# Values of two attentions projected 512 columns at a time, with the work around them re-ordered

## The chip, the cores and the metric

The kernel runs on one core of one Trainium2 chip. The metric is device time in microseconds (us) from launch to end, the median of the runs of one launch each; lower is better. Five engines work beside each other and wait for one another by semaphores: TensorE (PE in the profile; PEld its weight loads), VectorE (DVE), ScalarE (ACT), GpSimd (POOL) and SyncE (SP), which here issues all DMAs.

## What is computed

Two layers over 512 tokens of width 1024, in float32. Layer A is differential attention (8 heads, each the difference of two softmaxes, with rotary positions and a block-causal mask), layer B is chunked band attention (16 heads, with a learned bias by distance). Each is followed by a SwiGLU FFN of hidden width 2816, and every sub-layer ends in a LayerNorm of alpha * x + sublayer(x).

```python
def diff_attention(x, w_qkv, ...):
    q, k, v = split(x @ w_qkv)                 # each 512 x 1024
    a = softmax(q1 k1) - lam * softmax(q2 k2)  # per head and 128-query block
    o = rms_norm(a @ v, subln_g) * (1 - lambda_init)
    return o @ w_o
def chunk_attention(x, k_band, v_band, ...):
    q = x @ w_q
    p = softmax(q k_band + bias[h])            # own chunk and 8 before
    return (p @ v_band) @ w_o
def reference(x, ...):
    for l in range(2):
        x = layer_norm(alpha * x + attention_l(x))
        x = layer_norm(alpha * x + (silu(x @ w_gate) * (x @ w_up)) @ w_out)
```

k and v of layer B come from one projection of x by `kv_w`.

## The kernel before, in words

**Precision.** Every product of a projection is made of three matmuls: each operand is split into a high part (rounded to fp32r by ScalarE, or a cast while a bank is read out) and a low part (the rest, by VectorE's or POOL's subtraction), and high x high, high x low and low x high are summed in one PSUM bank. `token_major` (L407) has activations stationary and weights moving, `feature_major` (L397, for q, k, gate and up) the other way round.

**Weights.** All weight chunks stand in one list (`order`, L290 to 342), each 512 KB, 1024 values in each of 128 partitions. Five raw buffers are loaded ahead by `fetch` (L350) in that order, on SP's queue. `take` (L385) hands out a chunk and lets the split run up to two chunks ahead (`AHEAD`, L41), with at most four split chunks alive (`NSPL`, L40); `free` (L391) releases one. A chunk's low part is made by VectorE, or by POOL where the plan says so (the later values of both attentions, the later k of B).

**PSUM.** Eight banks of 512 float32 columns, in four pairs by tag: `sc0`, `sc1`, `sm`, `pj`. A new tile of a tag takes the bank used longest ago and waits until its readers are done.

**Order on the engines.** Nothing is scheduled by the program: a model of times (`Model`, L98; `passed`, L184) keeps an estimate of when each tile is ready, and work of VectorE, ScalarE and POOL that hangs on TensorE is written into the program when the model's clock gets there (`later`, `chain`, `tick`). Each engine then runs its instructions in the order written.

**The attention loops.** `attention_a` (L1106) and `attention_b` (L1351) go through 32 units (8 heads or pairs of heads x 4 query blocks), each in steps by `STEPS` and `STEPS_B` (L50, L52): scores, then softmax on VectorE and ScalarE, then the transposes of the probabilities (`at`), then the product with the values (`o`, or `v` once per pair in B). Between steps `weave` (L247) puts in filler: `FA` and `FB` (L49, L53) say how many ns of filler at which step, and where a step's inputs are not ready by the model, filler is pulled forward. Filler is the list `FILL_A` or `FILL_B` (L327, L328): the projections of later q and k ("qk") and of the values ("v", `value_fill` L840), then the first half of the output projection (`project_out`, L456). Its first 36 matmuls (row tiles 0 and 1, k 0 to 5, in the `pj` banks) need no more than the heads that are done; those of row tiles 2 and 3 take the `sc0` banks of the scores and wait for `gate(-1)`, which is `done["s"]`, set at the last unit's scores (L1123, L1370). In A q and k of head h start no sooner than unit 4(h-2) is scored, and are turned by rotary tables, which sends them through a DMA within SBUF. In B, q and k of pair p are read out, and filler goes on, once unit 4(p-1) is scored (L1224).

**Values.** `value_quarter` (L819) projects 256 of the 1024 value columns: for each of four row tiles 8 k x 3 matmuls of 256 columns, two row tiles sharing one bank. Quarter 0 of A comes with the input's transposes (L993 to 1029), then q and k of head 0, then quarter 1 (L1031); quarters 2 and 3 are filler. In B quarter 0 comes between the first and second halves of q and k of pair 0 (L1232 to 1245), the other three are filler.

**Transposes.** `transpose_split` (L412) transposes one row tile of 128 tokens into two `sm` banks (8 transposes) and reads each out as high part (ScalarE), low part (VectorE) and, where an FFN follows, as a whole into `hb` (ScalarE). In `swiglu` (L529) those of row tiles 2 and 3 are put between the first matmuls of gate and up, as soon as their LayerNorm is done by the model; first halves (tokens 0 to 255) of hidden units 0 and 1 run in `sc0` and `sc1`, then their second halves, unit 0's in the two `pj` banks (L788).

Of the kernel before, what the change touches and what calls it, by code (L numbers as in the profile page):

```python
# [19 lines left out]
P = 128  # L20
# [32 lines left out]
FB = ((1780.0, 1360.0, 0.0), (630.0, 2250.0, 100.0), 12, (2600.0, 0.0, 5250.0))  # L53
# [80 lines left out]
def trunk(ctx, tc, x, a_w_qkv, a_lambda, a_subln_g, a_w_o, kv_w, b_w_q, b_rel_bias, b_w_o,  # L134
# [684 lines left out]
    def value_quarter(g, banks, name):  # L819

        ws = [take(f"{name}_{g}_{c}") for c in range(2)]

        def part(i):
            for t in (2 * i, 2 * i + 1):
                b = banks[i][:, (t % 2) * 256:(t % 2) * 256 + 256]
                for k in range(KT):
                    ts_ = slice(t * P, (t + 1) * P)
                    w_ = ws[k // 4]
                    token_major(b, xTh[:, k, ts_], xTl[:, k, ts_], w_[0][:, k % 4, :], w_[1][:, k % 4, :],
                                k == 0, k == KT - 1)  # L830
                    if t == NT - 1 and k % 4 == 3:
                        free(f"{name}_{g}_{k // 4}")
                    yield True
            for t in (2 * i, 2 * i + 1):
                act_e.copy(vt[t][:, g * 256:(g + 1) * 256], banks[i][:, (t % 2) * 256:(t % 2) * 256 + 256])
            if i:
                values_done[0] = g + 1
        return part(0), part(1)
# [61 lines left out]
    for t in range(NT):  # L900
# [5 lines left out]
        if t < 2:  # L906
            fetch()
# [85 lines left out]
    vbank = [b_[:, 0:256] for b_ in pair("va_ps0") + pair("va_ps1")]  # L993

    def first_values(t, c, w_):
        ts_ = slice(t * P, (t + 1) * P)
        for i, (x_, v_) in enumerate(((xTh, w_[0]), (xTl, w_[0]), (xTh, w_[1]))):
            for j in range(4):
                mm(vbank[t], x_[:, 4 * c + j, ts_], v_[:, j, :], start=(c == i == j == 0),
                   stop=(c == 1 and i == 2 and j == 3))  # L1000

    transpose_split(xin[0], 0)
    tick(True)
    w0 = take("va_0_0")
    tick(True)
    transpose_split(xin[1], 1)
    tick(True)
    w1 = take("va_0_1")
    tick(True)
    first_values(0, 0, w0)  # L1010
    first_values(1, 0, w0)
    transpose_split(xin[2], 2)
    tick(True)
    first_values(0, 1, w1)
    first_values(1, 1, w1)
    transpose_split(xin[3], 3)
    tick(True)
    state["ahead"] = AHEAD
    for t in (2, 3):
        for c, w_ in ((0, w0), (1, w1)):  # L1020
            first_values(t, c, w_)
    free("va_0_0")
    free("va_0_1")
# [3 lines left out]
    for t in range(NT):  # L1027
        act_e.copy(vt[t][:, 0:256], vbank[t])
    values_done[0] = 1
    now(qk_a(0))  # L1030
    now(value_fill(1, "va"))  # L1031
# [74 lines left out]
    def attention_a():  # L1106
# [3 lines left out]
        for i in range(nu + max(step[1] for step in STEPS if step[0] != "fill")):  # L1110
            rates = FA[0] if i < FA[2] else FA[1] if i < nu else FA[3]
            for kind, n in STEPS:
# [6 lines left out]
                if kind == "s":  # L1119
# [3 lines left out]
                    done["s"] = i == nu - 1  # L1123
# [114 lines left out]
    for i, _ in enumerate(v0[0]):  # L1238
        tick()
        if not vt and (there(xres[3], late=LATP) or i == 2 * KT - 1):  # L1240
            pre_b[1](None)
            for t in range(NT):
                vt.append(resid.tile([P, D], F32, tag="res", name=f"vb_{t}"))
# [195 lines left out]
```

## Time and profile before

| | us |
|---|---|
| median of 3 runs | 1223.04 (1220.2 to 1223.32) |
| the profiled execution | 1223.91 |
| its span, first to last instruction | 1222.1 |
| TensorE busy | 1188.6 (97%) |
| VectorE busy | 834.2 (68%) |
| ScalarE busy | 555.8 (45%) |
| POOL busy | 417.1 (34%) |

One execution was recorded. Its stages, by the timeline: input transposes, values, q and k of head 0 to 47.9 us; attention A to about 236; the rest of its output projection and LayerNorm to 259.7; FFN of A to 612.4; attention B's projections ahead of the loop to 651.3, its loop to 832.1, the rest of its output projection to 863.8; FFN of B to the end. Matmuls are pipelined, so the duration of one (some 0.28 us for 256 columns) is longer than the distance to the next; the distance is read from pieces of the chain or from starts.

### The profile page before, as it was taken

To read this page: it belongs to the slowest core of one execution; us is meant where nothing else is said; L and a number is where in the kernel's file an instruction comes from. 1 tells how busy PE (TensorE), PEld (TensorE's weight loads), DVE (VectorE), ACT (ScalarE), POOL (GpSimd) and SP (SyncE) were. 2 spreads that over 40 slices of the span, in tenths; PEclk is the share of its full clock that TensorE was granted. 3 is DMA by queue.
4 is the path that set the end of the run, shared out by engine and by line. 5 is a ranking of instruction groups with operands and counts; after the bars stand their busy time and mean duration, and the time that the engine had idled before them with its cause. 6 is when DMAs were issued, how large, how long until landed. Compare 5 with 4: busy or idle time off the path is not lost.

```text
span 1222.1 us, 20005 instructions
## 1 busy us (share of the span) xinstructions
PE 1188.6 (97%) x7640; PEld 1079.4 (88%) x7640; DVE 834.2 (68%) x1451; ACT 555.8 (45%) x1049; POOL 417.1 (34%) x410
## 2 busy tenths in 40 slices
PE   7999999999999999999999999999999999999997
PEld 7878897789999999888897988978899999998886
DVE  3588786587888887432655676775888888873327
ACT  3467666344544444322236576662444444433220
POOL 1126343513555663001213243113236665510022
PEclk9999999999999999999999999999999999999999
DMA  8444233543544443424254233225433333353321
GB/s 258 126 107 120 65 105 93 173 131 98 148 141 140 139 133 119 162 88 138 86 146 122 86 105 112 80 78 189 122 104 104 104 105 104 106 191 100 104 69 69
DMA packets 164193, 145.75 MB, mean 119 GB/s; under 512 B 6097, under 2 KB 137457, under 8 KB 164097
## 3 DMA queue, kind: packets, MB, share of 16 engines
q1 hardware_dynamic: 164096, 144.47, 39.2%
q8 instruction: 60, 0.98, 0.3%
q14 instruction: 37, 0.30, 0.1%
HBM read 127.63 MB, written 13.67 MB: 116 GB/s over the span
## 4 chain that ended last, share of the span: by engine, by line
PE 90%; DVE 5%; issue 1%; DMA 1%; ACT 1%; POOL 1%; SPq 0%; DVEq 0%; POOLq 0%; ACTq 0%
PE m L198 31%; PE c L198 5%; PE a L198 5%; PE b L198 5%; PE gu L198 5%; PE d L198 4%; PE va_ps L198 4%; PE vb_ps L198 4%; PE bq_ps L198 3%; PE bk_ps L198 3%; PE q_ps L198 3%; PE k_ps L198 3%; PE ob L198 2%; PE po L198 2%; PE sc_b L198 2%; PE pt_b L203 1%
## 5 line engine op out<-in xcount | busy, mean ns | idle before, releaser
L76 POOL TENSOR_TENSOR sums<-raw_u 128x512 f32<-128x512 f32 x38 | 49.0, 1290 | 184.0 <-DVE s3lo L76 166.6
L76 ACT ACTIVATE sg<-sg 128x512 f32<-128x512 f32 x38 | 24.0, 633 | 189.6 <-DVE sg L76 189.6
L76 POOL TENSOR_TENSOR lo_fo<-raw_fo,hi_fo 128x1024 fp32r<-128x1024 f32 x8 | 19.1, 2388 | 217.3 <-ACT hi_fo L76 217.3
L76 POOL TENSOR_TENSOR sums<-raw_g,sums 128x512 f32<-128x512 f32 x38 | 84.6, 2226 | 0.0
L76 DVE TENSOR_TENSOR m<-m,m 128x256 f32<-128x256 f32 x76 | 31.7, 417 | 57.9 <-PE m L198 57.9
L76 ACT CAST hi_fk<-raw_fk 128x1024 fp32r<-128x1024 f32 x28 | 29.4, 1052 | 76.1 <-PE d L198 71.1
L76 DVE TENSOR_TENSOR lo_fk<-raw_fk,hi_fk 128x1024 fp32r<-128x1024 f32 x28 | 33.9, 1221 | 26.9 <-ACT hi_fk L76 26.9
L76 POOL TENSOR_TENSOR sums<-sums,raw_g 128x512 f32<-128x512 f32 x38 | 49.7, 1308 | 4.0 <-DMA raw_g<-in_ffn_w_in_dram 1.2
L76 POOL TENSOR_TENSOR sums<-raw_g,raw_u 128x512 f32<-128x512 f32 x38 | 50.9, 1340 | 0.0
L76 DVE TENSOR_TENSOR s1lo<-sums,s1hi 128x1024 fp32r<-128x1024 f32 x38 | 47.6, 1252 | 0.0
L76 DVE TENSOR_TENSOR alo<-raw_g,ahi 128x1024 fp32r<-128x1024 f32 x38 | 47.0, 1236 | 0.0
L76 ACT CAST hi_fo<-raw_fo 128x1024 fp32r<-128x1024 f32 x16 | 16.9, 1054 | 64.5 <-PE d L198 64.5
L76 DVE TENSOR_TENSOR s3lo<-sums,s3hi 128x1024 fp32r<-128x1024 f32 x38 | 46.0, 1212 | 0.1
L76 ACT CAST s3hi<-sums 128x1024 fp32r<-128x1024 f32 x38 | 40.0, 1052 | 8.3 <-POOL sums L76 4.6
L198 PE MATMUL m<-T1h,s1hi 128*128 128x256 f32 x152 | 43.0, 283 | 0.0
L198 PE MATMUL m<-T1l,s1hi 128*128 128x256 f32 x152 | 43.0, 283 | 0.0
L198 PE MATMUL m<-T1h,s1lo 128*128 128x256 f32 x152 | 43.0, 283 | 0.0
L198 PE MATMUL m<-T2g,s1hi 128*128 128x256 f32 x152 | 43.0, 283 | 0.0
L198 PE MATMUL m<-T2b,s1hi 128*128 128x256 f32 x152 | 43.0, 283 | 0.0
L198 PE MATMUL m<-T2g,s1lo 128*128 128x256 f32 x152 | 43.0, 283 | 0.0
L198 PE MATMUL m<-T3h,s3hi 128*128 128x256 f32 x152 | 43.0, 283 | 0.0
L198 PE MATMUL m<-T3l,s3hi 128*128 128x256 f32 x152 | 43.0, 283 | 0.0
(612 smaller groups left out, 4772.4 us busy)
## 6 DMA issues: line engine op xcount, KB each, us to landing
raw_g<-in_ffn_w_in_dram SPq DMA_DIRECT2D x44, 512.0 KB, 4.0
raw_u<-in_ffn_w_in_dram SPq DMA_DIRECT2D x44, 512.0 KB, 5.2
raw_fk<-in_ffn_w_out_dram SPq DMA_DIRECT2D x28, 512.0 KB, 4.0
raw_fo<-in_ffn_w_out_dram SPq DMA_DIRECT2D x16, 512.0 KB, 3.7
skew<-extd SPq DMA_DIRECT2D x16, 320.0 KB, 5.9
raw_va<-in_a_w_qkv_dram SPq DMA_DIRECT2D x8, 512.0 KB, 4.8
raw_q<-in_a_w_qkv_dram SPq DMA_DIRECT2D x8, 512.0 KB, 5.1
raw_k<-in_a_w_qkv_dram SPq DMA_DIRECT2D x8, 512.0 KB, 4.7
```

The lines of the kernel that those rows point to most:

```text
L76: return issue(*args, **kwargs)
L198: nc.tensor.matmul(out_, lhsT, rhs, start=start, stop=stop)
L203: nc.tensor.transpose(out_, in_, ident)
```

## The change

Values are projected 512 columns at a time ("half") in both attentions: `values` takes the place of `value_quarter`, a half's weights come as four chunks of 2 k x 512 columns in place of two of 4 k x 256, and each row tile has a bank of its own. Half 0 of each attention is computed ahead of its loop, half 1 is filler after q and k of head or pair 4. Beside that:

- A's first values: the loads alternate x tile, value chunk four times, and the first values' matmuls (`value_piece`, chunk by chunk) are placed between the transposes of the four x tiles. No values lie between q and k of head 0 and the loop.
- B's first values are placed chunk by chunk too: chunks 0 and 1 for row tiles 0 to 2, with tile 3's transposes among them, then the second halves of q and k of pair 0, then the rest.
- `transpose_split` uses the `pj` banks, not `sm`, for row tile 3 where an FFN follows.
- `done["s"]` is set at the last unit's `at` step, not at its scores.
- `FILL_A` and `FILL_B` end with q and k of 5, 6 and 7; `FB` is lowered by some 10%.

```diff
-FB = ((1780.0, 1360.0, 0.0), (630.0, 2250.0, 100.0), 12, (2600.0, 0.0, 5250.0))
+FB = ((1600.0, 1250.0, 0.0), (550.0, 2050.0, 100.0), 12, (2600.0, 0.0, 5250.0))
...
-        for c in range(2):
-            chunk(f"{name}_{g}_{c}", w, 4 * c, 4, c0 + g * 256, 256, pool)
+        for c in range(4):
+            chunk(f"{name}_{g}_{c}", w, 2 * c, 2, c0 + g * HALF, HALF, pool)
...
-    FILL_A = [("qk", 1), ("qk", 2), ("qk", 3), ("qk", 4), ("v", 2), ("qk", 5), ("qk", 6), ("v", 3), ("qk", 7)]
-    FILL_B = [("qk", 2), ("v", 1), ("qk", 3), ("qk", 4), ("v", 2), ("qk", 5), ("qk", 6), ("v", 3), ("qk", 7)]
+    FILL_A = [("qk", 1), ("qk", 2), ("qk", 3), ("qk", 4), ("v", 1), ("qk", 5), ("qk", 6), ("qk", 7)]
+    FILL_B = FILL_A[1:]
     plan_values("va", w_qkv, 2 * D, 0)
     plan_qk_a(0)
-    plan_values("va", w_qkv, 2 * D, 1)
...
-            pt = bank("sm", f"xt_ps_{t}_{g}")
+            pt = bank("pj" if whole and t == NT - 1 else "sm", f"xt_ps_{t}_{g}")
...
+    def values(g, name, parts, bank_of):
+        ws = []
+        def part(ts):
+            banks = [bank_of(t) for t in ts]
+            for t, b in zip(ts, banks):
                 for k in range(KT):
+                    if k % 2 == t == 0:
+                        ws.append(take(f"{name}_{g}_{k // 2}"))
...
+            for t, b in zip(ts, banks):
+                act_e.copy(vt[t][:, g * HALF:(g + 1) * HALF], b)
...
+    def value_piece(b, t, c, w_):
+        ts_ = slice(t * P, (t + 1) * P)
+        for i, (x_, v_) in enumerate(((xTh, w_[0]), (xTl, w_[0]), (xTh, w_[1]))):
+            for j in range(2):
+                mm(b, x_[:, 2 * c + j, ts_], v_[:, j, :], start=(c == i == j == 0), stop=(c == 3 and i == 2 and j == 1))
     def value_fill(g, name):
-        banks = [bank("pj", f"{name}_ps{i}_{g}") for i in range(2)]
-        for p_ in value_quarter(g, banks, name):
+        for p_ in values(g, name, [[t] for t in range(NT)], lambda t: bank("pj", f"{name}_ps{t}_{g}")):
             yield from p_
...
-        if t < 2:
-            fetch()
+        fetch()
...
+    first_x(0)
+    first_w()
+    first_x(1)
+    first_values(0, 0)
+    first_w()
+    first_values(1, 0)
+    first_x(2)
+    first_values(0, 1)
+    first_values(1, 1)
+    first_w()
+    first_values(2, 0)
+    first_x(3)
+    first_values(2, 1)
+    for t in range(3):
+        first_values(t, 2)
+    first_w()
...
-    now(value_fill(1, "va"))
...
-                    done["s"] = i == nu - 1
...
+                if kind == "at":
+                    done["s"] = i - n == nu - 1
...
+    for c in range(2):
+        first_values_b(c, range(3))
+    if not vt:
+        last_tile()
     now(first)
+    for c in range(4):
+        first_values_b(c, range(3 if c < 2 else 0, NT))
+        free(f"vb_0_{c}")
...
-                    done["s"] = i == nu - 1
                     done["n"] = i + 1
                 elif kind == "at":
                     yield lambda: there(live[i - n][1])
+                    done["s"] = i - n == nu - 1
```

## Rows read from the trace of the kernel before

**Rows 1.** The page, part 1: busy us, share of the span, instructions.
```profile
PE 1188.6 (97%) x7640; PEld 1079.4 (88%) x7640; DVE 834.2 (68%) x1451; ACT 555.8 (45%) x1049; POOL 417.1 (34%) x410
```

**Rows 2.** Windows: stretch, length, busy us by engine, granted clock, DMA share, GB/s.
```profile
267.30:269.50 2.20, 0.25 (x2) 0.05 (x1) 2.14 (x3) 0.61 (x2) 0.00 (x0) 1.00 0.99 256
270.50:273.90 3.40, 3.40 (x18) 3.40 (x17) 2.06 (x4) 3.11 (x6) 0.92 (x1) 0.50 1.16 292
...
655.50:661.80 6.30, 4.95 (x25) 3.37 (x24) 4.03 (x15) 3.63 (x15) 1.79 (x4) 1.00 0.15 46
...
651.30:717.90 66.60, 65.25 (x383) 56.70 (x382) 45.67 (x127) 44.71 (x115) 23.04 (x36) 1.00 0.33 99
...
651.30:832.10 180.80, 176.47 (x1051) 155.65 (x1050) 128.16 (x345) 118.33 (x305) 52.69 (x90) 0.99 0.30 91
```

**Rows 3.** Waits of TensorE: us in total, times, longest.
```profile
PE xt_ps L203 <- DMA xin<-in_x_dram: 6.7, 2, 3.6
PE xt_ps L203 <- ACT hb L76: 3.9, 2, 2.0
PE ob L198 <- DVE klb_b L76: 2.6, 1, 2.6
...
PE sc L198 <- DMA ks<-ks: 1.7, 1, 1.7
```

**Rows 4.** The chain of waits in order of time: start, us, what.
```profile
25.53 5.58 PE q_ps L198 x24
...
36.69 11.39 PE va_ps L198 x96
...
236.36 10.88 PE oa_1a L198 x48
```

**Rows 5.** Timeline, both FFNs' beginnings: start, us, instruction, count [idle before <-releaser].
```profile
268.88 1.18 ACT L76 COPY hb<-xt_ps 128x512 f32<-128x512 f32 x2 [6.45 <-DVE xTl_a L76]
...
269.52 1.40 PE L203 MATMUL xt_ps<-ident,oa_x 128*128 128x128 f32 x8 [1.97 <-ACT hb L76]
...
271.65 1.07 ACT L76 CAST xTh_a<-xt_ps 128x512 fp32r<-128x512 f32 x2
...
272.99 1.18 ACT L76 COPY hb<-xt_ps 128x512 f32<-128x512 f32 x2 [0.27 <-DVE xTl_a L76]
...
277.48 0.28 PE L198 MATMUL gu<-xTh_a,hi_g 128*128 128x256 f32 x1
...
877.07 1.19 ACT L76 COPY hb<-xt_ps 128x512 f32<-128x512 f32 x2 [0.27 <-DVE xTl_b L76]
...
881.59 0.28 PE L198 MATMUL gu<-xTh_b,hi_g 128*128 128x256 f32 x1
```

**Rows 6.** Timeline of TensorE at the start; DMA traffic of the first 16 us.
```profile
12.11 1.05 PE L198 MATMUL va_ps<-lo_va,xTh_a 128*128 128x256 f32 x4
12.97 1.05 PE L198 MATMUL va_ps<-hi_va,xTh_a 128*128 128x256 f32 x4
...
DMA packets 4243, 4.46 MB, mean 279 GB/s; under 512 B 157, under 2 KB 3475, under 8 KB 4243
```

**Rows 7.** Timeline of TensorE where the second attention begins.
```profile
621.60 1.25 PE L203 MATMUL xt_ps<-ident,fx 128*128 128x128 f32 x8 [1.24 <-DVE xTl_b L76]
```

**Rows 8.** Instructions that split value weights: durations ns min/median/max, first and last start.
```profile
L76 POOL TENSOR_TENSOR lo_va<-raw_va,hi_va x4: 2374/2508/2840, 99.2 to 154.9; 128x1024 fp32r<-128x1024 f32 x4
...
L76 ACT CAST hi_vb<-raw_vb x8: 1033/1054/1063, 611.3 to 757.2; 128x1024 fp32r<-128x1024 f32 x8
```

**Rows 9.** Timeline after the last scores of the first attention, TensorE and VectorE.
```profile
218.71 0.50 PE L198 MATMUL oa<-hi_oa,oTh 128*128 128x512 f32 x1 [1.46 <-DVE nm L76]
...
220.69 0.75 DVE L76 SCALAR_TENSOR_TENSOR e<-e,c 128x512 f32<-128x512 f32 x1
```

**Rows 10.** Timeline of TensorE after the last scores of the second attention.
```profile
822.40 0.48 PE L198 MATMUL ob<-hi_ob,oTh 128*128 128x512 f32 x1
...
826.58 0.60 PE L203 MATMUL pt_b<-ident,e_b 128*128 128x128 f32 x4
```

More of the change, by code (lines that the diff above doesn't have):

```diff
@@ L817, in trunk @@
     values_done = [0]
[L819 to L825, printed above, removed]
+    def values(g, name, parts, bank_of):
[3 more added lines that the diff above has]
+            for t, b in zip(ts, banks):
                 for k in range(KT):
+                    if k % 2 == t == 0:
+                        ws.append(take(f"{name}_{g}_{k // 2}"))
                     ts_ = slice(t * P, (t + 1) * P)
-                    w_ = ws[k // 4]
-                    token_major(b, xTh[:, k, ts_], xTl[:, k, ts_], w_[0][:, k % 4, :], w_[1][:, k % 4, :],
+                    w_ = ws[k // 2]
+                    token_major(b, xTh[:, k, ts_], xTl[:, k, ts_], w_[0][:, k % 2, :], w_[1][:, k % 2, :],
                                 k == 0, k == KT - 1)
-                    if t == NT - 1 and k % 4 == 3:
-                        free(f"{name}_{g}_{k // 4}")
+                    if t == NT - 1 and k % 2:
+                        free(f"{name}_{g}_{k // 2}")
                     yield True
-            for t in (2 * i, 2 * i + 1):
-                act_e.copy(vt[t][:, g * 256:(g + 1) * 256], banks[i][:, (t % 2) * 256:(t % 2) * 256 + 256])
-            if i:
+            for t, b in zip(ts, banks):
+                act_e.copy(vt[t][:, g * HALF:(g + 1) * HALF], b)
+            if t == NT - 1:
                 values_done[0] = g + 1
-        return part(0), part(1)
+        return [part(ts) for ts in parts]
+    def value_piece(b, t, c, w_):
[3 more added lines that the diff above has]
+                mm(b, x_[:, 2 * c + j, ts_], v_[:, j, :], start=(c == i == j == 0), stop=(c == 3 and i == 2 and j == 1))
     def value_fill(g, name):
-        banks = [bank("pj", f"{name}_ps{i}_{g}") for i in range(2)]
-        for p_ in value_quarter(g, banks, name):
+        for p_ in values(g, name, [[t] for t in range(NT)], lambda t: bank("pj", f"{name}_ps{t}_{g}")):
             yield from p_
@@ L990, in trunk, with first_values, first_x, first_w @@
     lead = ap1.tile([HB, 255], F32, name="lead")
[L993 to L1017, printed above, removed]
-    state["ahead"] = AHEAD
[L1019 to L1023, printed above, removed]
+    vbank = pair("va_ps0") + pair("va_ps1")
+    wv = []
+    def first_values(t, c):
+        value_piece(vbank[t], t, c, wv[c])
+    def first_x(t):
+        transpose_split(xin[t], t)
+        tick(True)
+    def first_w():
+        wv.append(take(f"va_0_{len(wv)}"))
+        tick(True)
+    first_x(0)
[14 more added lines that the diff above has]
+    first_w()
+    state["ahead"] = AHEAD
+    for c in range(3):
+        first_values(3, c)
+        free(f"va_0_{c}")
+    for t in range(NT):
+        first_values(t, 3)
+    free("va_0_3")
     vt = []
@@ L1235, in trunk, with last_tile, first_values_b @@
     values_done[0] = 0
-    v0 = value_quarter(0, pair("vb_ps_0"), "vb")
-    vt = []
[L1238 to L1243, printed above, removed]
-    now(first)
-    now(v0[1])
+    vbank = pair("vb_ps_0") + pair("vb_ps_1")
+    wv, vt = [], []
+    def last_tile():
+        pre_b[1](None)
+        for t in range(NT):
+            vt.append(resid.tile([P, D], F32, tag="res", name=f"vb_{t}"))
+    def first_values_b(c, ts):
+        if len(wv) == c:
+            wv.append(take(f"vb_0_{c}"))
+        for t in ts:
+            value_piece(vbank[t], t, c, wv[c])
+            if not vt and there(xres[3], late=LATP):
+                last_tile()
+    for c in range(2):
+        first_values_b(c, range(3))
+    if not vt:
+        last_tile()
+    now(first)
+    for c in range(4):
+        first_values_b(c, range(3 if c < 2 else 0, NT))
+        free(f"vb_0_{c}")
+    for t in range(NT):
+        act_e.copy(vt[t][:, 0:HALF], vbank[t])
+    values_done[0] = 1
     now(qk_b(1))
@@ L1383, in attention_b @@
                     if qt == PREP_B:
-                        yield lambda: 2 * values_done[0] > p
+                        yield lambda: 4 * values_done[0] > p
                         split_values(p)
```

4 lines of the change are left out of this document (2 added, 2 removed).

## The prediction, made before the changed kernel was built or run

> **What bounds the kernel now.** The page first: TensorE is busy for 97% of a span of 1222.1 us [rows 1]. Matmuls overlap in those records, so what counts is where TensorE stands still and how far apart its matmuls start. The waits of TensorE give the first [rows 3]: 6.7 us on the first input tiles, 3.9 on ScalarE's copies out of the transposes' banks, 2.6 on `klb_b`, 1.7 on `ks`. The windows give what a wait costs afterwards [rows 2]: after 2.2 us of almost no TensorE work the clock granted from 270.5 to 273.9 is 0.50, the lower of its two levels (1.2 of 2.4 GHz). 3.4 us at half rate do 1.7 us less work. So a wait of about 2 us costs nearer 4. The chain of waits gives the second [rows 4]: 96 matmuls of 256 columns take 11.39 us, 118.6 ns each; 48 of 512 columns whose moving operand is a weight take 10.88 us, 226.7 ns each; 24 of a q or k projection take 5.58 us, 232.5 ns each.
>
> **Values in halves.** Per attention 4 quarters x 4 row tiles x 8 k x 3 = 384 matmuls of 256 columns become 192 of 512. 384 x 118.6 ns = 45.5 us; 192 x 226.7 ns = 43.5 us; 2.0 us less, as TensorE is the bound here. Both attentions: **-4.1 us**. I take 226.7, because the new matmul is built as that one is (activations stationary, weights moving). At 232.5 ns the gain would be 0.9 us each: bounds -4.1 and -1.8. The bytes stay the same; the 16 evacuations of 256 columns become 8 of 512 and lie on ScalarE, off the path.
>
> The Trainium skill (TensorE: Matmul & The Clock Gate, Back-to-back issue gap) puts isolated warm matmuls at N/2.4 + 2.5 ns apart, 109.2 and 215.8 ns. By that the gain would be an estimated 0.5 us per attention and the sum 3.1 us higher. The trace's spacing is wider by 9.4 ns at 256 columns and 10.9 at 512; no run here shows why, and I go by the rows.
>
> **The last transposes of each FFN's input.** Now both tiles' transposes (tiles 2 and 3) go to the two `sm` banks, so those of tile 3 wait until tile 2 has been read by ScalarE, VectorE and ScalarE again: `hb` copies from 268.88 for 1.18 us, transposes at 269.52 [rows 5]. With `pj` for tile 3 they start when TensorE gets there, at 267.3. Eight take 0.9 us (ending 268.2). Then the rest of unit 1's first half: 48 - 3 = 45 matmuls x 0.119 = 5.4 us, ending 273.6, with no wait ahead that brings the low clock. What is late next: the second halves write to those same `pj` banks, and start only when tile 3 has been read out. ScalarE's order is fixed (hb of tile 2, table load, silu, xTh at 271.65, hb at 272.99 for 1.18 in two copies), hangs on VectorE (the releaser in the row of 268.88) and not on the transposes, so the first bank is free at 273.6, the second at 274.2, and that one is needed 24 matmuls later. The second halves start at 277.48 now, at about 273.65 then: -3.8 us. The second FFN has the same: from 881.59 to about 877.75 (first of the `hb` copies done at 877.07 + 0.59): -3.8. Together **-7.7 us**. Bounds: none if the wait only moves to the `pj` bank with another fall of the clock (0); -7.9 if the copies come a little earlier.
>
> **First loads and first values.** TensorE runs without a break from the second input tile's transposes on; up to about 14.5 us at half rate (four matmuls in 12.97 - 12.11 = 0.86 us, 215 ns each, against 118.6 later [rows 6]). The new order keeps x0, a value chunk, x1, a value chunk, x2 at the head and slips one 512 KB load ahead of x3; at the mean 279 GB/s of the first 16 us [rows 6] this is 1.9 us, and x3 is wanted later too (more work lies ahead of it). I take 0; between -1 and +2 (x3 late). SP's queue has the same number of loads. Quarter 1 no longer lies between q0, k0 and the first scores, where its 11.4 us [rows 4] hid the rotary chain; the 48 matmuls of q1 and k1 (11.2 us) come there instead, being the first filler.
>
> **Start of the second attention.** The transposes of tile 3 wait 1.24 us on the `sm` banks after 3 matmuls [rows 7]; in the new order at least 6 of 512 columns (1.4 us, against 0.36) come between: **-0.9**. Bounds -1.2 and +1 (tile 2's low part is wanted by the third piece already).
>
> **The later half as filler: a new wait.** A half holds four weight chunks of which two are split ahead. The third and fourth are begun only when the first and second are taken; splitting one is 1.05 us on ScalarE and 2.5 us on POOL [rows 8]. From the start of the half the third is ready after some 4.5 us and wanted after 12 x 0.227 = 2.7 us of filler plus the attention matmuls woven in; the fourth after some 7 and wanted after 4.1. Behind the waiting matmul stands all of TensorE, since it works in order. Woven in it is 0.8 us per attention, in one piece 2.8; at best none. I take **+1.6** in all (0 to +5.6).
>
> **Filler in the second attention's loop.** Quarter 1 leaves the loop for the time ahead of it. Filler of pair p stops after its q until unit 4(p-1) is scored. Quarter 1 used to lie between k2 and q3 and carried the loop past the gates of p = 3 and 4. Without it units 6 and 10 run out of filler. Units without filler cost TensorE 6.30 - 4.95 = 1.35 us in 655.5 to 661.8 [rows 2]; and VectorE's 45.67 us in the first twelve units would stand in some 55 us in place of 66.6 once the quarter's 11.4 us go, 83% of the time, not 69, so that a late unit is made up more slowly. I take **+1.5** (0 to +5).
>
> **Score banks, last q and k.** In the first attention the output projection's second half of row tiles now waits for the last transposes, not the last scores. Now its first matmul stands 1.46 us on `nm` (218.71), after which 12 matmuls run before the last `e` is ready at 220.69 + 0.75 [rows 9]. Then nothing fills that gap: 12 x 0.227 = 2.7 us of work come later, 1.5 of waiting goes: +1.1. The last q and k come 1.3 us of filler earlier, which takes some 0.6 off the 1.7 us on `ks`: **+0.5** together (-3.4 if that wait falls short and the clock stays up; +3 with another fall). In the second attention the 2.6 us on `klb_b` is `ob`'s second bank waiting for the last k to be read out; k still comes straight ahead of it, so it stays. Of the 18 matmuls between 822.40 and 826.58 [rows 10] only what is left of the first row tiles can run: up to 15 x 0.227 = 3.4 us uncovered, some of it covered by filler left over from the gates. I take **+1.0** (-4.3 with the wait and its low clock gone, +5.1 with all uncovered and one more fall).
>
> **Sum.** -4.1 - 7.7 - 0.9 + 1.6 + 1.5 + 0.5 + 1.0 = -8.1 us on the profiled execution's 1223.9 (span 1222.1 and 1.8 around it): 1215.8. The median of the runs is 0.9 lower, so **1215**.
>
> **Rivals.**
> *Tails heal too.* The waits on `ks` and `klb_b` both vanish, with their low clocks: 1.7 + 1.7 + 2.6 + 1.7 = 7.7 less, 1207. For it: both hang on when the last k ends, and that moves. Against: k is still followed at once by `oa` and `ob`.
> *The transposes' wait only moves.* The second halves wait for `pj` long enough to lose the 7.7: 1222. For it: the bank is free just when it is wanted, and whatever VectorE does 1 us later is paid in full. Against: 0.1 us of overlap is enough.
> *The second attention's loop does not shrink.* It must lose 12.4 us to pay for 10.4 more ahead of it; my sum has it lose 9.9. If VectorE's and ScalarE's chain holds it so that it loses 4, the time is 1221.
> *Slower:* the same loop starves at three places (units 6, 10 and after the last scores), each for over 2 us, so that each brings a 1.7 us loss to the low clock, and none of the 12.4 us comes back: 9.9 + 5.1 = 15 us on top of 1215, 1230. It decides where the loop from the first scores to the last value product, 180.8 us now with VectorE busy for 128.2 of them [rows 2], keeps 180 or more. Against: that leaves room for at least some of the 12.4.
>
> **How the numbers follow.** Forecast 0.60 (its own range 1210 to 1219), tails heal 0.14, wait moves 0.10, loop half stuck 0.10, slower 0.06. What can be told from no change is 0.3%, 3.7 us: below 1219.4 is faster, above 1226.7 slower. Faster: nearly all of the first two and a little of the fourth, 0.74; slower 0.06; the rest, 0.20, the same. The range of 8 in 10: 1206 to 1222.
>
> **What would show it.** Value matmuls 226.7 ns apart and 192 of them. No `hb` wait of `xt_ps`, full clock in the first row of gate and up, second halves 3.8 us closer to the start of the FFN. A wait of `va_ps` or `vb_ps` on POOL's `lo`. The second attention's loop at some 171 us. Wrong it is if gate and up start their second halves behind a `pj` wait of more than 1 us, if value matmuls lie at 232 ns, or if TensorE's waits inside the two loops add up to over 10 us.

## The result and the profile after

The changed kernel takes 1238.4 us (1235.7 to 1240.5) against 1222.6 for the kernel before beside it: a ratio of 1.0129, 95% interval 1.011 to 1.0148. It is 15.8 us slower; 1215, in a range of 1206 to 1222, was predicted. The profiled execution took 1238.7 us with a span of 1236.9.

The page's part 1 of the changed kernel answers to [rows 1]: TensorE runs 384 matmuls fewer, yet it is busy for 1190.7 us, not less than the 1188.6 before, and its share of the longer span falls to 96%.

```profile
PE 1190.7 (96%) x7256; PEld 1056.6 (85%) x7256; DVE 879.6 (71%) x1453; ACT 554.2 (45%) x1033; POOL 421.8 (34%) x408
```

Its waits (engine, line, releaser: us in total, times, longest) answer to [rows 3]. The `hb` wait is gone. Waits that belong to the units of the attention loops have grown: on `sq` from 2.2 to 6.7 us, on `e` from 1.5 to 4.6, on `e_b` from 1.2 to 3.4, on `ot` from 0.3 to 2.4, and one on `aT` is new.

```profile
PE xt_ps L203 <- DMA xin<-in_x_dram: 6.9, 2, 3.6
PE ot L203 <- DVE sq L76: 6.7, 5, 1.9
PE at L203 <- DVE e L76: 4.6, 6, 1.5
PE pt_b L203 <- DVE e_b L76: 3.4, 2, 2.1
PE ob L198 <- DVE klb_b L76: 3.2, 1, 3.2
PE o L198 <- ACT aT L76: 3.2, 3, 1.5
PE pt_b L203 <- DVE ot L76: 2.4, 4, 1.5
PE xt_ps L203 <- DVE ob_x L76: 1.8, 1, 1.8
...
PE vb_ps L198 <- POOL lo_vb L76: 1.1, 1, 1.1
```

The same waits in the kernel before:

```profile
PE ot L203 <- DVE sq L76: 2.2, 4, 1.0
PE at L203 <- DVE e L76: 1.5, 1, 1.5
PE pt_b L203 <- DVE e_b L76: 1.2, 1, 1.2
PE pt_b L203 <- DVE ot L76: 0.3, 1, 0.3
```

Windows of the changed kernel (stretch, length, busy us by engine, granted clock, DMA share, GB/s) answer to [rows 2]. In the first loop up to unit 28 TensorE is busy for 142.5 of 155.0 us.

```profile
61.50:216.50 155.00, 142.54 (x736) 115.18 (x736) 122.74 (x310) 98.65 (x276) 60.56 (x95) 1.00 0.35 94
...
224.20:234.50 10.30, 7.89 (x28) 6.58 (x29) 5.78 (x21) 5.38 (x18) 2.60 (x8) 0.50 0.01 2
...
818.20:825.00 6.80, 6.06 (x20) 5.38 (x21) 4.36 (x11) 2.83 (x8) 0.00 (x0) 0.50 0.35 103
273.00:300.00 27.00, 26.64 (x217) 26.02 (x216) 23.29 (x26) 11.67 (x17) 8.40 (x5) 1.00 0.49 135
```

The same stretch of the kernel before, first scores to unit 28, in the same columns, has 154.5 of 160.2; two rows below it are its spells at the low clock near the ends of the two loops.

```profile
47.90:208.10 160.20, 154.54 (x895) 132.80 (x894) 126.79 (x322) 104.14 (x289) 61.68 (x96) 1.00 0.37 101
...
209.10:212.40 3.30, 3.30 (x16) 3.13 (x15) 1.66 (x8) 2.19 (x9) 0.93 (x3) 0.50 0.00 0
...
806.40:809.80 3.40, 3.40 (x16) 3.21 (x15) 1.40 (x6) 0.63 (x2) 0.00 (x0) 0.50 0.34 116
```

So the idle time there went from 5.7 to 12.5 us. The spells at the low clock by the end of the two attentions grew from some 3.4 us each to 10.3 and 6.8 us at 0.50, while the beginning of the first FFN now has the full clock.

The stages, by the starts of the first matmul of each kind on TensorE (one profiled execution each, us; runs below are named by their labels):

| | to first scores of A | A: scores to `oa_1a` | to `bq` | to first scores of B | B: scores to `ob_1a` | to the last matmul |
|---|---|---|---|---|---|---|
| before | 47.9 | 188.3 | 376.2 | 38.9 | 188.9 | 373.8 |
| changed | 61.4 | 187.3 | 373.0 | 48.8 | 186.1 | 372.2 |
| e1_gate | 62.1 | 185.5 | 372.5 | 48.7 | 180.8 | 369.9 |
| e2_pj | 45.9 | 186.6 | 372.6 | 38.8 | 189.0 | 369.8 |
| e4_light | 62.3 | 181.0 | 372.7 | 48.8 | 179.9 | 369.9 |
| e3_order | 61.1 | 184.5 | 372.7 | 48.8 | 189.4 | 369.8 |
| e8_nocover | 51.2 | 185.5 | 374.7 | 38.9 | 189.0 | 373.7 |
| e11_ahead | 62.2 | 181.2 | 374.7 | 50.2 | 182.9 | 372.1 |
| e14_noswap | 57.6 | 184.6 | 373.1 | 48.8 | 186.9 | 373.9 |
| e17_rates | 61.9 | 185.6 | 372.5 | 48.8 | 182.6 | 369.8 |
| e18_rates_order | 61.4 | 180.9 | 372.5 | 48.7 | 187.2 | 370.0 |
| e19_pj_gate | 46.9 | 193.6 | 372.6 | 38.8 | 191.3 | 369.9 |
| e21_lo_short | 61.6 | 183.9 | 372.7 | 48.8 | 183.1 | 369.9 |
| e22_before_lo_short | 46.2 | 186.8 | 376.2 | 38.9 | 186.5 | 373.6 |

Like columns of like runs vary by up to 2 us: the first is 45.9 to 47.9 in the kernel before, e2, e19 and e22, whose work there is the same, while the fourth hardly varies. A profiled execution can also lie off the median of its runs: e4's is 3.5 us above, e14's 3.4, e19's 2.9 and e17's 1.9, e18's 3.7 below. Two kernels had one far longer execution each (3008.8 us in e6_b_half, the one that was recorded, and 2924.7 in e4_light), which their times below leave out.

Read by the columns, 13.5 us more lie ahead of the first loop, which got 1.0 shorter; 9.9 more lie ahead of the second, which got 2.8 shorter. The two FFN columns won 4.8. What lies ahead of the first loop is work: from the end of head 0's k to the first scores TensorE runs 63 matmuls of q1, k1 and q2 without a gap.

```profile
46.80:61.50 14.70, 14.70 (x65) 11.71 (x63) 10.47 (x16) 8.66 (x13) 3.56 (x3) 1.00 0.60 162
```

How a unit's wait can arise shows one of the five on `sq`, where the later half begins. POOL and VectorE of the changed kernel, timeline (start, us, instruction, count [idle before]):

```profile
116.21 2.38 POOL L76 TENSOR_TENSOR lo_va<-raw_va,hi_va 128x1024 fp32r<-128x1024 f32 x1 [0.96 <-ACT hi_va L76]
118.57 0.62 POOL L76 TENSOR_SCALAR ms<-ms 128x1 f32<-128x1 f32 x1
119.28 0.55 POOL L76 TENSOR_TENSOR rr<-ms,mexp 128x1 f32<-128x1 f32 x1
```

```profile
116.27 2.87 DVE L76 TENSOR_TENSOR krc<-kr,cosb 128x512 f32<-128x512 f32 x1
119.07 0.34 DVE L76 SCALAR_TENSOR_TENSOR sq<-o,rr,gsub 128x128 f32<-128x128 f32 x1
```

And TensorE beside them, the last filler matmul and the next unit's transpose:

```profile
117.18 0.40 PE L198 MATMUL va_ps<-hi_va,xTl_a 128*128 128x512 f32 x1
119.46 0.33 PE L203 MATMUL ot<-ident,sq 128*128 128x128 f32 x1 [1.89 <-DVE sq L76]
```

The `sq` that TensorE waits for stands on VectorE behind `krc`, which takes 2.87 us beside POOL's `lo_va`; the next unit's `ms` stands behind `lo_va` on POOL. TensorE's row names only the last of these. It is one case: `krc` took that long only here (the median of its eight is 0.69 us).

### The profile page after: what moved, and what is told of

The parts are those of the page before. It is cut to its first block, busy times and chain, and to the rows that moved or that the text cites. A ratio compares the mean times of both kernels' runs of the same rounds, so it can differ in the third digit from the quotient of the medians.

```text
span 1236.9 us, 19219 instructions
## 1 busy us (share of the span) xinstructions
PE 1190.7 (96%) x7256; PEld 1056.6 (85%) x7256; DVE 879.6 (71%) x1453; ACT 554.2 (45%) x1033; POOL 421.8 (34%) x408
## 5 line engine op out<-in xcount | busy, mean ns | idle before, releaser
L76 POOL TENSOR_TENSOR sums<-raw_g,sums 128x512 f32<-128x512 f32 x38 | 75.4, 1984 | 0.0
L76 POOL TENSOR_TENSOR sums<-raw_g,raw_u 128x512 f32<-128x512 f32 x38 | 68.8, 1811 | 0.0
L76 DVE TENSOR_TENSOR alo<-raw_g,ahi 128x1024 fp32r<-128x1024 f32 x38 | 66.9, 1761 | 0.0
L76 DVE TENSOR_TENSOR ulo<-raw_u,uhi 128x512 fp32r<-128x512 f32 x38 | 46.7, 1228 | 0.0
L76 DVE TENSOR_TENSOR s3lo<-sums,s3hi 128x1024 fp32r<-128x1024 f32 x38 | 46.1, 1213 | 0.1
L76 ACT ACTIVATE e_b<-e_b,mx_b 128x128 f32<-128x128 f32 (+3 forms) x64 | 35.6, 560 | 18.3 <-DVE mx_b L76 18.2
L76 POOL TENSOR_TENSOR rs<-rs,mexp 128x1 f32<-128x1 f32 x16 | 15.8, 986 | 81.9 <-DVE rs L76 81.9
L76 DVE TENSOR_TENSOR m<-m,m 128x256 f32<-128x256 f32 x76 | 31.6, 416 | 16.5 <-PE m L198 16.4
```

What stands on the lines that cost most here:

```text
L76: return issue(*args, **kwargs)
```

## The experiments

**The parts.** The theory was that the gate (where `done["s"]` is set), the transposes and the loops are separate, and that a loop does not get back what is taken ahead of it; the rival, that TensorE's work bounds the loops.

e1_gate, on the changed kernel, in both loops:

```diff
+                    done["s"] = i == nu - 1
...
-                    done["s"] = i - n == nu - 1
```

> The changed kernel with done["s"] set at the last unit's scores again, in both attentions. In the changed kernel the clock is at half from 224.2 to 234.5 us and from 818.2 to 825.0 (10.3 and 6.8 us, against 3.4 and 3.4 before), and TensorE waits 2.3 us where the second attention's gate opens. Theory (both loops lost their filler, and the gate adds only to their ends): 3 to 8 us less than the changed kernel's 1238.4, so 1230 to 1235. Rival (the gate is the whole loss): 1223. Rival (the gate costs nothing, since the first row tiles' 36 matmuls are used up before): 1237 to 1239.

Measured: 1229.9, ratio to before 1.0065 (1.005 to 1.008); 8.5 us less than the changed kernel. The gate costs more than priced, and most of it in the second attention (loop 186.1 to 180.8, and 2.3 behind it, where the wait on `ob_x` has gone). In a window of this run the mean granted clock is 0.83 where the changed kernel had 0.50: the spell shrinks to 3.4 us (228.4 to 231.8). In the second attention there is none.

```profile
224.20:234.50 10.30, 7.55 (x34) 6.16 (x35) 6.53 (x23) 5.15 (x17) 1.86 (x6) 0.83 0.01 2
```

e2_pj, on the kernel before:

```diff
-            pt = bank("sm", f"xt_ps_{t}_{g}")
+            pt = bank("pj" if whole and t == NT - 1 else "sm", f"xt_ps_{t}_{g}")
```

> The kernel before with nothing but the transposes of row tile 3 ahead of an FFN in the other pair of banks. Theory (the prediction's step holds: 3.8 us in each FFN): 1215 against the kernel before's 1222.6. By the changed kernel's stages (3.1 us less in the first FFN, 1.7 less in the second): 1217 to 1218. Rival (the wait only moves to the second halves): 1221 to 1223.

Measured: 1213.4, ratio 0.9928 (0.9914 to 0.9943); 8.8 us less. The step holds, and no other form measured here is faster. The two FFN columns got 7.6 us shorter by it. Its window over the start of the first FFN has the full clock and no idle TensorE, where [rows 2] had 0.50; ScalarE's `hb` row has the same wait on VectorE's `xTl_a` as in [rows 5], but TensorE no longer waits for it.

```profile
257.00:285.00 28.00, 28.00 (x221) 27.24 (x222) 24.28 (x26) 11.97 (x18) 8.45 (x5) 1.00 0.46 125
```

```profile
265.30 1.19 ACT L76 COPY hb<-xt_ps 128x512 f32<-128x512 f32 x2 [6.45 <-DVE xTl_a L76]
```

e6_b_half: the first attention's functions, list and gate as in the diff's minus lines, everything else as in its plus lines.

```diff
-    plan_values("va", w_qkv, 2 * D, 0)
+    plan_quarters("va", w_qkv, 2 * D, 0)
     plan_qk_a(0)
+    plan_quarters("va", w_qkv, 2 * D, 1)
```

> First attention as in the kernel before (quarters, gate at the scores), second attention and transposes as in the changed kernel. Theory (the two attentions' losses are separate; by stages the first one lost 12.6 us, the second 7.0, and the two FFNs won 4.8): 1238.4 - 12.6 = 1225 to 1226. Rival (the loss of the first is partly something both share, such as the FFN's later loads): 1229 or more. If the second attention costs nothing by itself: 1218.

Measured: 1223.3, ratio 1.0001 (0.9991 to 1.0011). That is some 2 us below the theory's range: the first attention's part of the change costs 15.1 us, more than the 12.5 of its columns, and the rest 9.9 over e2_pj. Its trace is not used here.

e4_light, on the changed kernel, in `values`:

```diff
-                    token_major(b, ..., k == 0, k == KT - 1)
+                    if k % 2 == 0 and t == 0 or k == 0:
+                        token_major(b, ..., k == 0, k == (6 if t == 0 else 0))
```

> The changed kernel without 75 of the 96 matmuls of the later half of the values in each attention (its weights are still loaded and split, its banks read out; the values come out wrong in columns 512 to 1023). That takes 75 x 0.2267 = 17.0 us of TensorE work out of each loop, 34 in both. Theory (the loops are held by each unit's own chain of softmax, norm and transposes, so that work ahead of the loop is not given back inside it): less than half comes back, 1221 or more. Rival (TensorE's work bounds the loops, and the loss is one of order alone): three quarters or more, 1213 or less; 1204 in full.

Measured: 1221.0, ratio 0.9983 (0.9964 to 1.0002). Of the 17.0 us taken out of each loop 6.3 and 6.2 came back by the columns; by the medians, 1238.4 to 1221.0, it was 17.4 of 34.0 in the whole kernel, about half and at the theory's bound. TensorE then idles for 16.4 of 145.9 us in the first loop and 11.2 of 135.1 in the second:

```profile
62.40:208.30 145.90, 129.50 (x660) 105.26 (x661) 118.69 (x307) 95.35 (x269) 59.62 (x92) 0.96 0.36 100
664.90:800.00 135.10, 123.95 (x635) 102.63 (x634) 101.37 (x284) 94.92 (x247) 40.51 (x73) 0.97 0.33 96
```

So TensorE's work alone no longer bounds these loops: this speaks for the theory and against the rival, which wanted 1213 or less.

**What in the loops does it.**

e3_order:

```diff
-    FILL_A = [("qk", 1), ("qk", 2), ("qk", 3), ("qk", 4), ("v", 1), ("qk", 5), ("qk", 6), ("qk", 7)]
+    FILL_A = [("qk", 1), ("qk", 2), ("v", 1), ("qk", 3), ("qk", 4), ("qk", 5), ("qk", 6), ("qk", 7)]
```

> The changed kernel with the later half of the values ahead of q and k of 3 in both filler lists, not behind those of 4. In the changed kernel q and k of heads 5 and 6 run in one piece (161.4 to 182.1 us) because unit 20 waits for head 5, and the second attention's units 6 and 10 run without filler. Theory A (a list in the wrong order: the filler is there but comes in lumps): 5 to 9 us less than 1238.4, so 1229 to 1233. Theory B (work taken ahead of the loop can't be got back inside it, whatever the order): 1236 to 1240.

Measured: 1235.4, ratio 1.0104 (1.0083 to 1.0125), between the two. The first loop gains 2.8 us, the second loses 3.3, so the two lists want different orders.

e5_dve_lo:

```diff
-POOL_K, POOL_VA, POOL_VB, ... = False, True, True, False, True
+POOL_K, POOL_VA, POOL_VB, ... = False, False, False, False, True
```

> The changed kernel with the low parts of the later values made by VectorE (1.2 us a chunk), not POOL (2.4 us), in both attentions. Theory (POOL, which also makes the norm's root and the rotary product, holds up the unit's chain while it splits, and slows VectorE beside it: TensorE waits 6.7 us for sq and 1.4 for lo of the values): 2 to 4 us less than 1238.4, 1234 to 1236. Rival (VectorE is the fuller engine, and 8 x 1.2 us more on it delay the softmax): 1240 or more. If POOL's chain has nothing to do with it: 1237 to 1239.

Measured: 1239.6, ratio 1.0141 (1.0121 to 1.016): no gain. TensorE's waits in the first attention only change places. Of this run, from 47 to 250 us:

```profile
PE at L203 <- DVE e L76: 3.9, 6, 1.4
PE o L198 <- ACT aT L76: 3.7, 3, 1.9
PE ot L203 <- DVE sq L76: 3.7, 3, 1.9
PE va_ps L198 <- DVE lo_va L76: 1.8, 1, 1.8
```

e10_lag:

```diff
-STEPS = (("s", 0), ("fill", 0), ("o", 2), ("ot", 3), ...
+STEPS = (("s", 0), ("fill", 0), ("o", 2), ("ot", 4), ...
-        sq = new(ap2, 2, [P, P], F32, "sq", f"sq_{n_}")
+        sq = new(ap3, 3, [P, P], F32, "sq", f"sq_{n_}")
```

> The changed kernel with the transposes of a unit's output (ot) one unit later in the first attention's loop, and a third buffer for sq. If TensorE's waits there (6.7 us on sq, of 16.5 in that loop) are the latency of one unit's norm, exposed since less filler lies in between: they vanish, and 4 to 7 us go: 1231 to 1234. If the loop is held by the amount of work on VectorE, ScalarE and POOL, the waits move to at or o: 1237 to 1240.

Measured: 1238.3, ratio 1.0133 (1.0113 to 1.0153). The wait on `sq` is gone, and other links have it:

```profile
PE at L203 <- DVE e L76: 5.4, 5, 1.9
PE at L203 <- DVE oTl L76: 4.7, 2, 3.1
PE o L198 <- ACT aT L76: 3.9, 4, 1.9
```

e8_nocover, on the kernel before:

```diff
-    FILL_A = [("qk", 1), ("qk", 2), ("qk", 3), ("qk", 4), ("v", 2), ...
+    FILL_A = [("qk", 1), ("qk", 2), ("v", 1), ("qk", 3), ("qk", 4), ("v", 2), ...
...
-    now(value_fill(1, "va"))
```

> The kernel before, all in quarters, with nothing changed but the place of the first attention's quarter 1: out of the stretch between q and k of head 0 and the loop, into the filler between q and k of 2 and 3. Then q1, k1 and some of q2 cover the rotary chain of head 0, as in the changed kernel. Theory (the loss in the first attention is this place, not the size of the pieces): the loop does not get shorter by what moved ahead of it, 8 to 13 us more than the kernel before's 1222.3, so 1230 to 1235. Rival (halves, with their four chunks and a bank for each row tile, make the loss): 1221 to 1224.

Measured: 1223.1, ratio 1.0011 (0.9998 to 1.0025). The theory that the place alone makes the loss falls. The expectation was badly worked out, too: 14.6 us of q and k go ahead of the loop, but 11.4 us of values come into it, so only 3.2 net leave it, and the loop got 2.8 shorter: this small amount came back almost whole. What it leaves open is whether a loop gives back a larger amount.

**Amount or form, and the rotary exchange.**

e11_ahead, on the kernel before, in quarters, with `("v", 1)` taken out of `FILL_B`:

```diff
-    now(qk_a(0))
     now(value_fill(1, "va"))
+    now(qk_a(0))
...
     now(v0[1])
+    now(value_fill(1, "vb"))
     now(qk_b(1))
```

> The kernel before, all in quarters, with quarter 1 computed straight behind quarter 0 in both attentions: in the first, q1, k1 and some of q2 then cover head 0's rotary chain (14.6 us leave the loop), in the second, quarter 1's 11.4 us leave the loop. The work ahead of each loop is as large as in the changed kernel, in the old form and with the old gate. Theory A (work taken ahead of a loop is not got back inside it): some 12 us more in the first attention and 3 to 5 in the second, 1234 to 1240. Theory B (the form of the halves, with four chunks and 512 columns in a piece, makes the loss): 1221 to 1226.

Measured: 1232.8, ratio 1.0081 (1.0064 to 1.0098), 10.2 us over the kernel before and 1.2 short of Theory A's range. With the old form, banks and gate the larger amount ahead makes most of the loss: 14.3 us more ahead of the first loop give 7.1 back, 11.3 ahead of the second give 6.0. Part of what does not come back is the clock: each loop has 6.8 us at 0.50 (214.1 to 217.5 and 224.4 to 227.8; 814.9 to 821.7) in place of 3.4, which at half rate is an estimated 1.7 us of work more. In the first loop up to unit 28 TensorE is idle for 10.1 of 151.4 us, where the kernel before had 5.7 of 160.2:

```profile
62.40:213.80 151.40, 141.26 (x831) 120.57 (x831) 119.90 (x313) 98.09 (x279) 59.42 (x95) 1.00 0.36 97
```

e13_rope_dve, e14_noswap (both on the changed kernel) and e16_before_noswap (on the kernel before):

```diff
-            ... (lambda: [sw], lambda: pool_e.tensor_mul(sw, sw, sinb)) ...
+            ... (lambda: [sw], lambda: vec_e.tensor_mul(sw, sw, sinb)) ...    # e13
-                load_e.dma_start(sw[b * 32:(b + 1) * 32, :], ...)
+            ... (lambda: [r], lambda: pool_e.tensor_mul(sw, r, sinb)) ...     # e14, e16
```

> The changed kernel with the rotary product sw * sin on VectorE, not POOL. In the changed kernel POOL waits in order for the rotary exchange through a DMA (44 us of such waits inside the first loop, 22 in the kernel before) and the norm's root (ms, rr) of a unit stands behind it, so that TensorE waits 6.7 us for sq. Theory C (that queue is what starves TensorE): 4 to 8 us less than 1238.4, 1230 to 1234. Rival (VectorE then waits for the same DMA in its own order): 1238 to 1244.

> The changed kernel without the rotary exchange by DMA: the product is made from r itself (q and k of the first attention come out wrong; every other operation stays). Theory C (the exchange, and what queues behind it on POOL and VectorE, makes the first loop's waits): 8 to 12 us less than 1238.4, 1226 to 1231, all of it in the first loop. If the waits are of softmax and norm alone: 1236 to 1239.

> The kernel before without the rotary exchange by DMA (q and k of the first attention come out wrong). By Theory C the exchange costs it little, since more filler lies between: 1 to 3 us less than 1222.3, 1219 to 1221. If the exchange costs the two kernels the same, it is no cause of their difference.

Measured: e13 1240.6 (1.0148, 1.013 to 1.0167), e14 1231.4 (1.0075, 1.0052 to 1.0098), e16 1222.7 (1.0002, 0.999 to 1.0014). e13 only moves the wait for the exchange from one queue to another: TensorE's wait on `sq` fell from 6.7 to 2.0 us, but others took its place (up to 3.6 us at one `e`, 1.9 on `kr`), as the rival said. So it does not show what POOL's queue costs by itself. The exchange costs the changed kernel 7.0 us, somewhat less than Theory C's 8 to 12, and the kernel before nothing. By the columns 3.8 of it lie ahead of the first scores, where less of the loop's filler is spent as cover, and 2.7 in the loop. So this latency is free where the filler is ample and is paid for where the filler is short.

**The spread of the filler, the gate alone, a better form.** These six runs ask why a loop does not give back what leaves it.

e17_rates and e18_rates_order, both with e1's gate, e18 also with e3's order:

```diff
-FA = ((780.0, 2350.0, 630.0), ...
+FA = ((670.0, 2010.0, 540.0), ...
```

> The changed kernel with the gate at the scores again, and the first attention's filler rates lowered to what it has (670, 2010 and 540 ns in place of 780, 2350 and 630). Theory A (the rates spend the filler too early; the last units then run bare): 4 to 8 us less than the 1229.9 with the gate alone, 1222 to 1226. Theory B (the units' own chain holds the loop): 1228 to 1232.

> As the run with the gate at the scores and lower rates, and with the later half of the values ahead of q and k of 3 in both lists. Order alone took 3.0 us off the changed kernel. Theory A (spread and order are the loss): 1218 to 1223. Theory B (the chain holds the loop): 1226 to 1230.

Measured: 1229.2 (1.0048, 1.0029 to 1.0067) and 1234.4 (1.0088, 1.0071 to 1.0106). The rates do nothing. With the order the kernel is 5.2 us slower, outside of both expectations. By the columns the order takes 4.7 us off the first loop (185.6 to 180.9) and puts 4.6 on the second (182.6 to 187.2); they do not show the 5.2, since e17's profiled execution lies above its median and e18's below.

e19_pj_gate (e2 with the changed kernel's gate) and e20_pj_v3last (e2 with another order in the first attention):

```diff
-                    done["s"] = i == nu - 1
+                if kind == "at":
+                    done["s"] = i - n == nu - 1                               # e19
-    FILL_A = [..., ("qk", 5), ("qk", 6), ("v", 3), ("qk", 7)]
+    FILL_A = [..., ("qk", 5), ("qk", 6), ("qk", 7), ("v", 3)]                 # e20
```

> The kernel before with the transposes' edit and with the gate at the last unit's at step in both attentions. With the transposes alone it was 1213.4. If the gate costs the same in the old form as in the changed one (8.5 us, most of it in the second attention): 1220 to 1223. If its price hangs on the filler that the halves left over: 1214 to 1217.

> The kernel before with the transposes' edit, and with q and k of head 7 ahead of the last quarter of the first attention's values, so that 11.4 us more filler cover the last k's rotary chain. If the wait on ks (1.6 us) and the low clock after it go and nothing takes their place: 2 to 3.5 us less than 1213.4, 1210 to 1211.5. If the values then come late for head 6: 1214 to 1217.

Measured: 1220.1 (0.9981, 0.9972 to 0.9991) and 1213.4 (0.9925, 0.9907 to 0.9943). The gate costs 6.7 us in the old form as well, by the columns mostly in the first attention (186.6 to 193.6). Not all of these 7.0 us are the gate's: the first attention of e19's profiled execution has two spells of 3.4 us at 0.50, e2's has none, and one of the two, behind a wait on `ks`, is like that of the kernel before at 209.1. The other order changes nothing: the wait on `ks` is gone, but no low clock stood behind it in e2, and the wait on `e` went from 1.4 to 2.3 us.

e21_lo_short (on e1_gate) and e22_before_lo_short (on the kernel before):

```diff
+            few = shape[0] // 8 if key.lstrip("bqk") in list("234567") else shape[0]
-                a[0], a[1], a[2].bitcast(F32))), ...
+                a[0][:, :n], a[1][:, :n], a[2][:, :n].bitcast(F32))), ...
```

> The changed kernel with the gate at the scores, where the low part of the weights of q and k of 2 to 7 is made for one of eight k blocks only and that block stands in for all (q and k come out less exact; TensorE, ScalarE and the loads do the same work). About 1 us less for VectorE in each of 12 chunks of the first loop and 6 of the second, and less for POOL. Theory V (VectorE's queue holds the loops): 6 to 15 us less than the 1229.9 with the gate alone, 1215 to 1224. Rival L (the latency of a unit's chain through all engines holds them, not VectorE's amount of work): 1227 to 1231.

> The kernel before with the same low parts left out. There TensorE is the bound in the loops, so both theories expect little: 0 to 3 us less than 1222.7, 1219.5 to 1222.7. If it falls by as much as the changed one, VectorE's work costs both alike and is no cause of their difference.

Measured: 1230.3 (1.0073, 1.0048 to 1.0098) and 1218.5 (0.9976, 0.9963 to 0.9989). The gain of Theory V did not come. In the same stretch VectorE is busy for 115.3 us of 155.0, where e1 had 122.1 (window of e21, then of e1):

```profile
61.50:216.50 155.00, 144.10 (x745) 117.79 (x745) 115.29 (x314) 98.63 (x275) 59.47 (x95) 0.99 0.35 95
```

```profile
61.50:216.50 155.00, 141.81 (x732) 114.45 (x731) 122.10 (x309) 98.39 (x273) 59.95 (x95) 1.00 0.35 95
```

What VectorE gave up did not shorten the kernel: the first loop got 1.6 us shorter, the second 2.3 longer. This does not clear VectorE, though, for other things changed with it. TensorE's wait on `sq` fell (e1, then e21), and one on POOL's `lo_va`, 0.3 us in e1, grew to 3.9:

```profile
PE ot L203 <- DVE sq L76: 7.1, 6, 1.9
```

```profile
PE va_ps L198 <- POOL lo_va L76: 3.9, 2, 3.0
...
PE ot L203 <- DVE sq L76: 1.7, 3, 1.4
```

The granted clock was 0.50 for 13.6 us of e21's two attentions (124.3 to 127.7, 223.3 to 230.1, 817.2 to 820.6), against 3.4 us in e1; at half rate the 10.2 us more are an estimated 5.1 us of work. The kernel before, whose loops are fuller, gained 3.6, more than either theory's 0 to 3. An estimated 1.7 us of that is a spell at 0.50 in its second loop (806.4 to 809.8) that e22's profiled execution does not have.

## Why the prediction was wrong, point by point

**The step that failed** is that of the first values: that q1 and k1 come ahead of the first scores "being the first filler" was priced at 0, which takes for granted that the loop gets shorter by what leaves it. It was also more than the 48 matmuls named there: 63 went ahead. For the second loop the same was written as "it must lose 12.4 us ... my sum has it lose 9.9". For amounts of 11 to 17 us the runs show a return of about half at best: 7.1 of 14.3 and 6.0 of 11.3 (e11_ahead), 6.3 and 6.2 of 17.0 (e4_light; 17.4 of 34.0 by the medians). The kernel before stood where TensorE's work just filled the loop (154.5 of 160.2 us); filler there was cover for the units' chains as much as work, for which e4 and the pair e14 and e16 speak. The rival with that mechanism was bound to the second attention and to "180 or more" from its first scores to its last value product. That stretch came to 174.4 in the changed kernel, 6.4 shorter where the sum had 9.9. The larger loss was in the first attention, which the sum did not hold at all. A second term, the score banks, was mis-sized by some 7 us (below). Two signs that the prediction had named for being wrong are there: value matmuls 232 ns apart, and waits of TensorE inside the loops of over 10 us (16.2 on `sq`, `e`, `aT` and `oTl` in the first alone).

The first attention's two columns got 12.5 us longer. The amount ahead makes 7.2 of it (e11), the order of its list perhaps 4.7 (e17 to e18), the gate 1.8 (e1), and the values give back 0.9: 12.8. The second's got 7.1 longer: the gate 5.3 (e1), the amount 5.3 (e11), less 0.9 for the values and 0.8 at its start: 8.9. These sums come within 2 us, the spread of single profiles. The order is their weakest term: e3 against the changed kernel gives 2.8 for it, and no run sets the changed list against the old one.

**Values in halves**, -4.1: half of it. The new matmuls lie 232.3 ns apart (the mean distance of starts within the halves), not 226.7, so each attention saves 45.5 - 192 x 0.2323 = 0.9 us. That was the bound of -1.8. Four lines of the changed kernel's timeline show it, pairs 0.46 to 0.48 us apart:

```profile
21.62 0.62 PE L198 MATMUL va_ps<-hi_va,xTh_a 128*128 128x512 f32 x2
22.08 0.62 PE L198 MATMUL va_ps<-hi_va,xTl_a 128*128 128x512 f32 x2
22.54 0.63 PE L198 MATMUL va_ps<-lo_va,xTh_a 128*128 128x512 f32 x2
23.00 0.64 PE L198 MATMUL va_ps<-hi_va,xTh_a 128*128 128x512 f32 x2
```

The issue gap that the prediction cited from the Trainium skill (TensorE: Matmul & The Clock Gate, Back-to-back issue gap; 215.8 ns at 512 columns) is not seen here either; the measured distance decides.

**The transposes**, -7.7: right, -8.8 by e2_pj alone (-7.6 by its two FFN columns). In the changed kernel the chain of waits (start, us, what) runs through them in the second FFN with nothing between:

```profile
883.69 0.87 PE xt_ps L203 x8
884.57 5.81 PE gu L198 x48
890.37 0.87 PE xt_ps L203 x8
891.25 28.02 PE gu L198 x189
```

**First loads**, 0: right (the wait on `xin` 6.9, 6.7 before). **Start of the second attention**, -0.9: right, the wait on `xTl_b` went from 1.24 to 0.4 us. **The later half's wait on POOL's lo**, +1.6: right in size, 1.1 and 0.3 us. Other waits of the loop hid more of it: where a run relieved those, the wait on `lo_va` came to 3.1 us (e14) and 3.9 (e21).

**Filler gates in the second loop**, +1.5: units 5, 6, 9 and 10 do run without filler, but the change that fills them (e3_order) empties 13, 17 and 18 and made that loop 3.3 us longer, so their price stays open.

**Score banks**, +0.5 and +1.0: mis-sized, 8.5 in the changed form (e1) and 6.7 in the old (e19). The prediction counted the matmuls left uncovered, and one more fall of the clock only as the upper bound. It came in both attentions (10.3 and 6.8 us at 0.50 against 3.4 and none with the old gate), with a new wait of 2.1 us on `e_b`, and moved the LayerNorm that the next transposes need (the wait on `ob_x`).

**What stays open** is which link of a unit's chain sets the pace of a loop short of filler. Relieving VectorE's amount of work (e21), POOL's splits (e5), POOL's place in the rotary chain (e13), the step of `ot` (e10) or the rates (e17) alone did not shorten the kernel; in all but e17 the wait moved to another link. No run relieves two of them at once, so each may still be a part of it. That it is the latency of the whole chain, which fits e14 and e16, is argued, not shown. The lowered `FB` was not run alone either.

## What to carry to other kernels

Where one engine's work just fills a loop, work woven into that loop is also the cover for the other engines' latencies. Here 11 to 17 us of it came back by half or less when they left, and 3 us nearly whole: do not price such a move at nothing unless a run with that work left out shows the loop getting shorter by it. A wait that has one row in the table can move to another link of the same chain when it is removed; take the whole stretch's time as the measure. Test the parts of a bundled change alone: here one line won 8.8 us (ratio 0.9928 to the kernel before) and the rest lost 25.

## What the runs showed of the hardware beyond that

- Matmuls of 512 columns with a weight moving lie 232.3 ns apart in the halves, where 6 (first half) or 24 (later half) in a row go into one bank, and 226.7 in `oa_1a` [rows 4], where the bank changes every three. Many in a row into one bank do not by themselves bring the wider distance: near the end of the changed kernel 24 in a row into one bank take 5.44 us, 226.7 ns each (chain: start, us, what). What brings it stays open.

```profile
1212.94 5.44 PE b L198 x24
```

- VectorE's `krc`, two inputs in SBUF, took 2.87 us beside POOL's `lo_va` (116.21 to 118.59), 0.69 us at 73.86 without it. The Trainium skill (SBUF — State Buffer, Who interferes with whom) says that a VectorE instruction with two SBUF inputs contends with a GpSimd instruction that reads SBUF, and that the port pair they share is an exclusive lock. The trace agrees in this one case: `krc` begins 0.06 us after `lo_va` and ends 0.55 us after it.

```profile
73.86 0.69 DVE L76 TENSOR_TENSOR krc<-kr,cosb 128x512 f32<-128x512 f32 x1 [1.25 <-ACT kr L76]
```

- In both FFNs the same VectorE instruction `alo` took 1236 ns on average before and 1761 after, in both kernels beside POOL's `sums` for some 97% of its time, and TensorE did not wait for it. So the rise of VectorE's share (68% to 71%) is no sign of a cost there.
- In the changed kernel the granted clock from 224.2 to 234.5 us was 0.50, the lower of its two levels, with TensorE busy for 7.9 of the 10.3 us in the records; in the 7.7 us ahead of it, at the full clock, TensorE was busy for 5.3. Not every long wait is followed by such a spell: a wait of 3.2 us on `klb_b` was, from 818.2 us in the changed kernel, and was not in e1_gate (at 817.0), so the prediction's "a wait of about 2 us costs nearer 4" holds for some waits only.

```profile
216.50:224.20 7.70, 5.27 (x37) 4.22 (x35) 4.95 (x21) 4.13 (x19) 2.04 (x7) 1.00 0.01 2
```
